# A hybrid RWKV-7/Hyena block on one core: a fixed order of products in the first stage, low halves on VectorE, and low-rank weights a block ahead

## The chip, the cores and the metric

The kernel runs on one core of one Trainium2 chip. The metric is the time of one execution in microseconds (us). TensorE (PE) multiplies, VectorE (DVE), ScalarE (ACT) and GpSimd (POOL) work on elements, and SyncE (SP) issues most DMA transfers, GpSimd some.

## What is computed

A block of two layers on a latent sequence of 256 tokens and a context of 256 tokens, 2048 channels, float32. Layer 0 mixes tokens with RWKV-7, layer 1 with a Hyena convolution; a squared-ReLU MLP follows each. Only the front of layer 0 is touched here:

```python
mod  = (silu(c) @ ada_w[i] + ada_b[i])          # 6 x 2048; shift mod[0], scale mod[1]; modc from c_ctx
h    = modulate(rms_norm(x, norm_g), mod[0], mod[1])
xx   = shift_grid(h) - h                        # neighbour token, minus the token
xw, xk, xa = h + xx*mu[1], h + xx*mu[2], h + xx*mu[4]      # and mu[0], mu[3], mu[5] for r, v, gate
lw   = dec_w0 + tanh(xw @ dec_w1) @ dec_w2      # two directions, rank 96
a    = sigmoid(a0 + (xa @ a1) @ a2)             # two directions, rank 96
g    = sigmoid((h + xx*mu[5]) @ g1) @ g2        # latent only, rank 256
k, v, r = xk @ w_k, xv @ w_v, xr @ w_r          # 2048 x 2048
kk   = k*k_k ; kk = kk * rsqrt(sum(kk*kk, per head))       # then the scan over tokens
```

## The kernel before, in words

Channels lie on partitions, in 16 tiles k of 128; the 512 columns of a tile are 256 context and 256 latent tokens. A float32 product is made as three products of split halves (`mm3`): ScalarE casts the high half (`xh`, `wh`, `l2h`), a subtraction gives the low half (`xl`, `wl`, `l2l`), and PE adds high·high, low·high and high·low. `split_into` makes both halves; its `eng` says which engine subtracts, VectorE by default.

**First stage** (`start`, 0 to about 198 us). It needs shift and scale of layer 0, 2048 channels each, which come in four quarters q of 512 channels. `ada_first(ch, q)` loads eight weight tiles `aw` of 512 KB for one of the two, multiplies each with silu(c) on PE (L288), copies the sum (`rows`), turns it with the small `pick` products (L294), and VectorE adds the bias (`mod`, `modc`). `rwkv_h(q)` then scales four tiles of `hall` on ScalarE. For each of these k, `shifted` builds `sx` (shifted minus own token; ScalarE, then two VectorE additions), and `mix_split` builds four mixtures `xt` on VectorE (mu indices 1, 4, 5 and 2; index 5 on the latent half, 256 columns) with halves `xh` and `xl`. Indices 1, 4 and 5 go into the first low-rank products (12 `mm` and 6 `sg` matmuls a k); index 2 is kept for the product with w_k. `ONPOOL` puts all `xl` on GpSimd, through L172. In `start`, the order of an engine's queue is set by a scheduler with priorities (`high_priority`); code marked by pins (`self.pins`, `pin`) keeps the order in which it is written.

**Second stage** (`rwkv_proj`, to 457 us): the 2048 x 2048 product with w_k, and beside it 44 of the 80 units of `lora2`, the second low-rank products, the mixtures of r and v, and `ada_run`, the rest of layer 0's modulation (`aw` tiles of 256 KB, added up in `acc` on VectorE or GpSimd). For each of 16 row tiles the square `ksq` is split, `ksh` on ScalarE and `ksl` on GpSimd, and summed per head by two `sg` products (L743).

**Third stage** (`rwkv_begin`, 457 to 590 us): `scan_prepare(0)`, a chain of small steps that ends in an inverse by substitution (31 steps of `d` and `tmp` on VectorE), the fills of r and v (`fl` products; `fx` loaded from GpSimd's queue, `fr` from SyncE's), and the remaining 36 units of `lora2`, the last 16 of them the eight gate blocks. The scan's first products, `sc<-VU,NT`, follow. In `lora2` the tiles `raw`, `l2h` and `l2l` have one buffer each; a block's load, its two halves and its products follow one another.

Of the kernel before, what the change touches and what calls it, by code (L numbers as in the profile page):

```python
# [69 lines left out]
class Kern:  # L70
# [42 lines left out]
    pins = None  # L113

# [162 lines left out]
    def ada_first(self, ch, i, pool):  # L277
# [5 lines left out]
        for k in range(0, KT, 2):  # L283
            w = pool.tile([P, 2, 512], F32, name="aw", bufs=self.AW)
            nc.sync.dma_start(w, self.I["ada_w"][0, k * P : (k + 2) * P, c0 : c0 + 512].rearrange("(a p) n -> p a n", p=P))
            for a in range(2):
                j = (k + a) % 4
                nc.tensor.matmul(ps[32 * j : 32 * j + 32, :], lhsT=self.wide[:, k + a, :], rhs=w[:, a],  # L288
                                 start=k < 4, stop=k >= KT - 4, tile_position=(0, 32 * j))
# [3 lines left out]
        for b in range(4):  # L293
            nc.tensor.matmul(tp[:, b, :], lhsT=rows[:, b * P : (b + 1) * P], rhs=self.pick, start=True, stop=True)  # L294
# [3 lines left out]
    def ada_run(self, n, pool, psum="mm", on_pool=True, per=2, bufs=2):  # L298
# [308 lines left out]
    def rwkv_h(self, xp, q):  # L607

        nc = self.nc
        for st in range(2):  # L610
            hv = self.hview(st)
            gs = xp.tile([P, 16], F32, name=f"gs{st}", bufs=1)
            cs = slice(4 * q, 4 * q + 4)
            scl = self.modc[:, 1, cs] if st == 0 else self.mod[:, 0, 1, cs]
            nc.vector.scalar_tensor_tensor(gs[:, cs], scl, 1.0, self.col("norm_g", 4 * q, 4), op0=ALU.add, op1=ALU.mult)
            for k in range(4 * q, 4 * q + 4):
                sh = self.modc[:, 0, k : k + 1] if st == 0 else self.mod[:, 0, 0, k : k + 1]
                nc.scalar.activation(hv[:, k, :], hv[:, k, :], AF.Identity, scale=gs[:, k : k + 1], bias=sh)
# [60 lines left out]
    def lora2(self, pool):  # L679
# [5 lines left out]
        block = lambda: (pool.tile([P, 512], t, name=n, bufs=1) for t, n in ((F32, "raw"), (F32R, "l2h"), (F32R, "l2l")))  # L685
        for q in range(4):
            for nm, e in (("dec", 0), ("dec", 1), ("a", 0), ("a", 1)):
                b0 = self.hw0 if nm == "dec" else self.ha0
                r, hi, lo = block()
                nc.sync.dma_start(r[:RANK], I[f"{nm}_w2"][0, e][:, q * 512 : (q + 1) * 512])  # L690
                w = self.split_into(hi[:RANK], r[:RANK], lo[:RANK])
                for j in range(4):
# [3 lines left out]
                    t = pool.tile([P, 512], F32, name="l2t")  # L696
                    nc.scalar.activation(t, ps, AF.Tanh, scale=0.5, bias=b0[:, e * 16 + m : e * 16 + m + 1])
                    (nc.gpsimd if m % 4 < self.LPOOL else nc.vector).tensor_scalar(t, t, 0.5, 0.5, op0=ALU.mult, op1=ALU.add)
                    if nm == "dec":
                        u = pool.tile([P, 512], F32, name="l2u")  # L700
# [5 lines left out]
        for q in range(8):  # L706
            r, hi, lo = block()
            nc.sync.dma_start(r[:].rearrange("p (k n) -> p k n", k=2),
                              I["g_w2"][0][:, q * 256 : (q + 1) * 256].rearrange("(k p) n -> p k n", p=P))
            w = self.split_into(hi[:], r[:], lo[:])  # L710
            for j in range(2):
# [4 lines left out]
                t = pool.tile([P, 512], F32, name="l2t")  # L716
# [4 lines left out]
    def rwkv_proj(self, l2, ad1):  # L721
        nc, tc, I = self.nc, self.tc, self.I
        ev = self.ev
        ad = self.ada_run(self.ADA[0], ad1, "sg", self.ONP[0], 1, 2)
# [8 lines left out]
        def evk(m, ps):  # L733
# [7 lines left out]
            self.split_into(sh[:], s[:], sl[:], nc.gpsimd)  # L741
# [753 lines left out]
    ONPOOL = {1: 4, 4: 4, 5: 4, 2: 4}  # L1495
# [131 lines left out]
    def start(self, ap, xp):  # L1627
# [15 lines left out]
        for ch in range(2):  # L1643
            self.ada_first(ch, 0, ap)
        acc = [self.mm.tile([P, 512], F32, name="mm") for _ in range(4)]
        gacc = [self.sg.tile([P, 512], F32, name="sg") for _ in range(2)]
        for q in range(4):
            w, wg = weights(q)
            if q < 3:
                with self.tc.high_priority(self.PRA):  # L1650
                    for ch in range(2):
                        self.ada_first(ch, q + 1, ap)
            with self.tc.high_priority(self.PRH):
                self.rwkv_h(ap, q)
            self.xs = self.xs if q else []
            for k in range(4 * q, 4 * q + 4):
                sx = self.shifted(k)
# [177 lines left out]
```

## Time and profile before

| | |
|---|---|
| median of three runs | 3630.55 us (3610.51 to 3632.46) |
| profiled execution | 3626.62 us, its span 3623.9 us |
| PE busy | 3349.5 us (92%) |
| DVE, ACT, POOL busy | 2474.2 us (68%), 1740.7 us (48%), 551.9 us (15%) |
| mean granted PE clock | 0.965 of full speed |
| moved by DMA | 836.78 MB, mean 231 GB/s |

Times inside the span are counted from its start. Busy shares are means over stages of different kinds; the three stages above are the first 16% of the span.

### The profile page before, as it was taken

What the parts mean: (1) busy time and instruction counts of PE and PEld (TensorE: products, weight loads), DVE (VectorE), ACT (ScalarE), POOL (GpSimd) and SP (SyncE); (2) the same over time, 40 slices, a digit from 0 to 9 for tenths busy, and PEclk for the clock granted to TensorE, in tenths of its full rate; (3) what the DMA queues carried; (4) which work ended last, traced back from release to release, by engine and by line L of the source; (5) the groups of instructions that cost most, each with busy time, mean ns of one, the idle gap of its engine ahead of it and who ended that gap; (6) DMA issues with size and microseconds to landing.
All of it is one profiled execution on the core that took longest, in us unless ns stands there. A gap on an engine that the chain in (4) does not pass through costs nothing. (4 is left out here: it accounts for less than half of the span.)

```text
span 3623.9 us, 74582 instructions
## 1 busy us (share of the span) xinstructions
PE 3349.5 (92%) x30598; PEld 2912.4 (80%) x30598; DVE 2474.2 (68%) x3787; ACT 1740.7 (48%) x3069; POOL 551.9 (15%) x576
## 2 busy tenths in 40 slices
PE   7798877989999878999999999999999899999999
PEld 3376666878888756798988889899997798989897
DVE  5888675777777755587777776587787685555554
ACT  4444344444554544444434335576564664435343
POOL 2632221111111000000000002044441540000000
PEclk9989988999999989999999999999999999999999
DMA  9668798888899735688888887476665776555553
GB/s 328 203 211 268 238 293 253 272 267 272 272 281 276 224 126 168 202 257 288 255 271 277 283 264 240 158 238 214 213 211 176 241 251 197 178 189 182 192 181 126
DMA packets 587806, 836.78 MB, mean 231 GB/s; under 512 B 39551, under 2 KB 373280, under 8 KB 587464
## 3 DMA queue, kind: packets, MB, share of 16 engines
q1 hardware_dynamic: 556360, 718.76, 62.0%
q0 software_dynamic: 31104, 113.26, 9.9%
q8 instruction: 239, 3.92, 0.4%
q14 instruction: 103, 0.84, 0.1%
HBM read 777.31 MB, written 54.59 MB: 230 GB/s over the span
## 5 line engine op out<-in xcount | busy, mean ns | idle before, releaser
L53 DVE TENSOR_TENSOR wl<-w,wh 128x1024 fp32r<-128x1024 f32 (+1 forms) x716 | 919.6, 1290 | 541.1 <-ACT wh L53 537.8
L53 ACT CAST wh<-w 128x1024 fp32r<-128x1024 f32 (+1 forms) x716 | 737.7, 1043 | 728.8 <-PE mm L111 416.4
L111 PE MATMUL mm<-hxh,wh 128*128 128x258 f32 x2816 | 805.3, 287 | 13.2 <-DVE nt L53 11.4
L111 PE MATMUL mm<-hxh,wl 128*128 128x258 f32 x2816 | 803.9, 286 | 5.5 <-DVE wl L53 5.5
L111 PE MATMUL mm<-hxl,wh 128*128 128x258 f32 x2816 | 801.1, 285 | 0.0
L111 PEld LDWEIGHTS mm<-hxh,wh 128*128 128x128 f32 x2816 | 536.3, 191 | 17.4 <-DVE nt L53 13.5
L111 PEld LDWEIGHTS mm<-hxh,wl 128*128 128x128 f32 x2816 | 536.0, 190 | 8.5 <-DVE wl L53 7.2
L111 PEld LDWEIGHTS mm<-hxl,wh 128*128 128x128 f32 x2816 | 538.6, 191 | 1.8
L322 POOL TENSOR_TENSOR acc<-acc,aw 128x512 f32<-128x512 f32 x180 | 274.2, 1523 | 1360.7 <-ACT aw L53 1259.3
L111 PE MATMUL mm<-wh,uh 128*128 128x512 f32 x1024 | 405.8, 396 | 1.2 <-DVE nt L53 1.2
L111 PE MATMUL mm<-wl,uh 128*128 128x512 f32 x1024 | 400.2, 391 | 4.0 <-DVE wl L53 4.0
L111 PE MATMUL mm<-wh,ul 128*128 128x512 f32 x1024 | 402.6, 393 | 0.0
L53 DVE SCALAR_TENSOR_TENSOR acc<-aw,sc,acc 128x512 f32<-128x512 f32 x300 | 233.4, 778 | 101.0 <-DMA aw<-in_ada_w 98.5
L111 PEld LDWEIGHTS mm<-wl,uh 128*128 128x128 f32 x1024 | 192.6, 188 | 49.0 <-DVE wl L53 6.2
L111 PEld LDWEIGHTS mm<-wh,ul 128*128 128x128 f32 x1024 | 192.2, 188 | 45.6
L111 PEld LDWEIGHTS mm<-wh,uh 128*128 128x128 f32 x1024 | 192.6, 188 | 42.3 <-DVE nt L53 1.8
L111 PE MATMUL fl<-fh,fx 128*128 128x256 f32 x1024 | 213.1, 297 | 10.1 <-DMA fx<-xv 8.6
L111 PEld LDWEIGHTS fl<-fh,fx 128*128 128x128 f32 x1024 | 168.6, 194 | 28.1 <-issue 14.1
L53 ACT ACTIVATE aw<-aw,sc 128x512 f32<-128x512 f32 x180 | 125.7, 719 | 130.7 <-DMA aw<-in_ada_w 129.6
L111 PE MATMUL fl<-flo,fx 128*128 128x256 f32 x512 | 146.4, 286 | 0.0
L111 PE MATMUL mm<-xh,wh 128*128 128x512 f32 (+1 forms) x320 | 126.8, 416 | 17.5 <-ACT xh L53 14.1
L111 PE MATMUL sg<-ard,KB 64*64 64x64 f32 (+1 forms) x3584 | 130.4, 247 | 11.2 <-DVE NT L53 3.7
(352 smaller groups left out, 6016.3 us busy)
## 6 DMA issues: line engine op xcount, KB each, us to landing
aw<-in_ada_w SPq DMA_DIRECT2D x288, 512.0 KB, 5.7
w<-in_mlp_down SPq DMA_DIRECT2D x128, 1024.0 KB, 5.2
w<-in_mlp_up SPq DMA_DIRECT2D x120, 1024.0 KB, 6.1
fx<-xv POOLq DMA_DIRECT2D x128, 512.0 KB, 6.2
aw<-in_ada_w SPq DMA_DIRECT2D x192, 256.0 KB, 3.1
w<-in_hy_in_w SPq DMA_DIRECT2D x44, 1024.0 KB, 5.9
fx<-xr POOLq DMA_DIRECT2D x64, 512.0 KB, 5.8
w<-in_w_k SPq DMA_DIRECT2D x16, 1024.0 KB, 5.7
```

Source lines behind the costliest of these rows:

```text
L53: return self.kern.pin(self.key, f(*a, **kw))
L111: return self.pin("pe", self.nc.tensor.matmul(out, lhsT=lhsT, rhs=rhs, **kw))
L322: nc.gpsimd.tensor_tensor(acc, acc, w[:, a], op=ALU.add)
```

## The change

- The first stage is written so that PE's order is fixed (pins for PE alone): per k, up to six `aw` tiles of the next quarter and then the 18 products of k. `rwkv_h` yields after each k.
- `ONPOOL` becomes 0 for all, and `ksl` loses its `nc.gpsimd`: 64 `xl` and 16 `ksl` subtractions move from GpSimd to VectorE.
- `lora2` loads `raw` one block ahead, or two when its buffers are doubled; in `rwkv_begin` its tiles come from a pool of their own, "l2b", with two buffers for `raw`, `l2h`, `l2l` and three for `l2t`, `l2u`.
- `ada_run`'s loads in the second stage are issued under `issue_after(self.mixed)`, the last `xl` of the first stage.

```diff
@@ pin
-        if self.pins is not None:
+        if self.pins is not None and key in self.pinned:
@@ split_into
-        (eng or self.nc.vector).tensor_tensor(lo, f32, hi, op=ALU.subtract)
+        self.split_last = (eng or self.nc.vector).tensor_tensor(lo, f32, hi, op=ALU.subtract)
@@ ada_first: nc.tensor.matmul becomes self.product, and after each aw tile
+            yield
@@ ada_run
+                with self.tc.issue_after(behind) if behind else ExitStack():
+                    nc.sync.dma_start(w, ...)
@@ rwkv_h
+        for k in range(4 * q, 4 * q + 4):
+            for st in range(2):
...
+                nc.scalar.activation(hv[:, k, :], hv[:, k, :], AF.Identity, scale=gs[st][:, k : k + 1], bias=sh)
+            yield
@@ lora2
-        block = lambda: (pool.tile([P, 512], t, name=n, bufs=1) for t, n in ((F32, "raw"), (F32R, "l2h"), (F32R, "l2l")))
+        self.l2p = pool, 1
+        def blocks():
...
+            load(*todo.pop(0))
+            while raws:
+                r, n = raws.pop(0)
+                p, b = self.l2p
+                hi, lo = (p.tile([P, 512], F32R, name=nm, bufs=b) for nm in ("l2h", "l2l"))
+                w = self.split_into(hi[:n], r[:n], lo[:n])
+                while todo and len(raws) < b:
+                    load(*todo.pop(0))
+                yield w
@@ rwkv_proj
-            self.split_into(sh[:], s[:], sl[:], nc.gpsimd)
+            self.split_into(sh[:], s[:], sl[:])
@@
-    ONPOOL = {1: 4, 4: 4, 5: 4, 2: 4}
+    ONPOOL = {1: 0, 4: 0, 5: 0, 2: 0}
@@ start
+        self.pins, self.pinned = {}, ("pe",)
+        ada = lambda q: itertools.chain(self.ada_first(0, q, ap), self.ada_first(1, q, ap))
...
             for k in range(4 * q, 4 * q + 4):
+                with self.tc.high_priority(self.PRH):
+                    next(h)
+                with self.tc.high_priority(self.PRA):
+                    for _ in itertools.islice(nxt, 6 if k % 4 < 3 else 99):
+                        pass
                 sx = self.shifted(k)
...
+        self.mixed = self.split_last.ins
@@
-                self.rwkv_begin()
+                with ExitStack() as e3:
+                    self.l2p = self.pool(e3, "l2b", 3), 2
+                    self.rwkv_begin()
```

PE in the first stage, before: the last two `aw` tiles of quarter 3 (`aw_1059`, `aw_1063`) stand between the products of the last k of quarter 2 (`mm_369` to `sg_374` are the six sums).

```order
L288 MATMUL sc_1034<-aw_1059,wide_139 32x512 x2
L111 MATMUL sg_373<-xh_1255,wh_988 128x256
L111 MATMUL sg_374<-xh_1255,wh_988 128x256
L111 MATMUL mm_369<-xl_1230,wh_978 96x512
L111 MATMUL mm_369<-xh_1231,wl_979 96x512
L111 MATMUL mm_370<-xl_1230,wh_978 96x512
L111 MATMUL mm_370<-xh_1231,wl_979 96x512
L288 MATMUL sc_1034<-aw_1063,wide_139 32x512 x2
```

The same place after, from the last product of the second k of quarter 2:

```order
L111 MATMUL sg_374<-xh_1134,wl_989 128x256
L111 MATMUL sc_1088<-aw_1153,wide_139 32x512 x2
L111 MATMUL sc_1088<-aw_1157,wide_139 32x512 x2
L111 MATMUL sc_1088<-aw_1161,wide_139 32x512 x2
L111 MATMUL sc_1088<-aw_1165,wide_139 32x512 x2
L111 MATMUL sc_1171<-pick_143,rows_1169 128x2 x4
L111 MATMUL mm_369<-xh_1183,wh_978 96x512
L111 MATMUL mm_369<-xl_1182,wh_978 96x512
L111 MATMUL mm_369<-xh_1183,wl_979 96x512
```

The last four tiles of quarter 3 and the turn by `pick` now stand in one run, two k's of products ahead of the end of quarter 2, and the three products of a tile follow one another.

VectorE at the end of the first stage, before (`xt` mixtures, `sx` the shift; `acc` adds up layer 0's other modulation, which is work of the second stage):

```order
L53 SCALAR_TENSOR_TENSOR acc_1620<-aw_1659,sc2_92,acc_1620 128x512
L53 SCALAR_TENSOR_TENSOR xt_1413<-sx_1395,cols_71,hall_126 128x512
L53 TENSOR_TENSOR sx_1441<-sx_1441,hall_126 128x255
L53 TENSOR_TENSOR sx_1441<-sx_1441,hall_126 128x192
L53 SCALAR_TENSOR_TENSOR acc_1620<-aw_1730,sc2_92,acc_1620 128x512
L53 SCALAR_TENSOR_TENSOR xt_1425<-sx_1395,cols_71,hall_126 128x256
L53 SCALAR_TENSOR_TENSOR xt_1437<-sx_1395,cols_71,hall_126 128x512
L53 SCALAR_TENSOR_TENSOR acc_1620<-aw_1743,sc2_92,acc_1620 128x512
L53 SCALAR_TENSOR_TENSOR xt_1447<-sx_1441,cols_71,hall_126 128x512
L53 SCALAR_TENSOR_TENSOR acc_1620<-aw_1754,sc2_92,acc_1620 128x512
```

and after, up to the last `xl` (`wl` is a low half of w_k):

```order
L53 SCALAR_TENSOR_TENSOR acc_1622<-aw_1775,sc2_92,acc_1622 128x512
L53 SCALAR_TENSOR_TENSOR xt_1459<-sx_1441,cols_71,hall_126 128x512
L53 TENSOR_TENSOR xl_1433<-xt_1435,xh_1434 128x512
L53 SCALAR_TENSOR_TENSOR acc_1622<-aw_1870,sc2_92,acc_1622 128x512
L53 TENSOR_TENSOR xl_1445<-xt_1447,xh_1446 128x512
L53 SCALAR_TENSOR_TENSOR xt_1471<-sx_1441,cols_71,hall_126 128x256
L53 SCALAR_TENSOR_TENSOR acc_1622<-aw_1881,sc2_92,acc_1622 128x512
L53 TENSOR_TENSOR xl_1457<-xt_1459,xh_1458 128x512
L53 SCALAR_TENSOR_TENSOR xt_1483<-sx_1441,cols_71,hall_126 128x512
L53 TENSOR_TENSOR xl_1469<-xt_1471,xh_1470 128x256
L53 SCALAR_TENSOR_TENSOR acc_1622<-aw_1894,sc2_92,acc_1622 128x512
L53 TENSOR_TENSOR wl_1546<-w_1543,wh_1545 128x1024
```

The `xl` now stand in VectorE's queue behind their `xt`, and the `acc` additions still stand there among them, ahead of the last `xl`.

PE at the end of `rwkv_begin`, before: the last of three gate blocks (products of `hh_g`, `hl_g` with `l2h`, `l2l`, 12 a block) that stand between the last fill product and the scan.

```order
L111 MATMUL sc_5042<-hl_g0_1521,l2h_5007 128x256
L111 MATMUL sc_5012<-hh_g0_1522,l2l_5008 128x256
L111 MATMUL sc_5012<-hh_g1_1529,l2h_5007 128x256
L111 MATMUL sc_5012<-hl_g1_1528,l2h_5007 128x256
L111 MATMUL sc_5012<-hh_g1_1529,l2l_5008 128x256
L111 MATMUL sc_5042<-hh_g0_1522,l2l_5008 128x256
L111 MATMUL sc_5042<-hh_g1_1529,l2h_5007 128x256
L111 MATMUL sc_5042<-hl_g1_1528,l2h_5007 128x256
L111 MATMUL sc_5042<-hh_g1_1529,l2l_5008 128x256
L111 MATMUL sc_5161<-VU_5150,NT_5082 64x64 x8
```

and after, half a gate block and what follows it:

```order
L111 MATMUL sg_5089<-ard0_3605,KB_3705 64x64
L111 MATMUL sc_5045<-hh_g0_1522,l2h_5011 128x256
L111 MATMUL sc_5045<-hl_g0_1521,l2h_5011 128x256
L111 MATMUL sc_5045<-hh_g0_1522,l2l_5012 128x256
L111 MATMUL sc_5045<-hh_g1_1529,l2h_5011 128x256
L111 MATMUL sc_5045<-hl_g1_1528,l2h_5011 128x256
L111 MATMUL sc_5045<-hh_g1_1529,l2l_5012 128x256
L111 MATMUL sg_5088<-ard0_3605,KB_3705 64x64 x2
L111 MATMUL sg_5089<-ard0_3605,KB_3705 64x64
L111 MATMUL sg_5090<-ard0_3605,KB_3705 64x64
L111 MATMUL fl_4774<-fx_5003,fh_4999 128x256 x2
L111 MATMUL fl_4774<-fx_5003,flo_5000 128x256
```

Behind the last row come three more such fill groups, four of the next fill, and then `sc_5165<-VU_5154,NT_5086`. Gate products now stand between fills (`fl`), and none in a row ahead of the scan; from the end of the inverse (`d,d`) to the scan PE has 48 fill and 18 gate products after, 24 and 48 before, and 24 of `ard`, `KB` in both.

## Rows read from the trace of the kernel before

**Rows 1.** Busy time by stretches in the first stage; columns: stretch, length, busy us of PE, PEld, DVE, ACT, POOL (instructions), granted PE clock, DMA share, GB/s.

```profile
50.00:100.00 50.00, 47.27 (x243) 20.18 (x239) 36.14 (x49) 27.64 (x51) 29.39 (x21) 0.97 0.94 317
...
150.00:200.00 50.00, 29.46 (x101) 18.41 (x100) 41.44 (x51) 25.49 (x42) 27.20 (x18) 0.70 0.41 120
```

**Rows 2.** VectorE in order of time, 50 to 200 us: each quarter's `mod`; columns: start us, us, instruction [idle before <- releaser].

```profile
52.54 0.16 DVE L53 TENSOR_TENSOR mod<-sc,cols 128x4 f32<-128x4 f32 x1 [8.84 <-PE sc L294]
...
83.06 0.15 DVE L53 TENSOR_TENSOR mod<-sc,cols 128x4 f32<-128x4 f32 x1
...
113.64 0.15 DVE L53 TENSOR_TENSOR mod<-sc,cols 128x4 f32<-128x4 f32 x1
...
154.47 0.16 DVE L53 TENSOR_TENSOR mod<-sc,cols 128x4 f32<-128x4 f32 x1
```

**Rows 3.** Groups of instructions by line and shape, 0 to 200 us; columns: busy us, mean ns of one, idle before and releasers.

```profile
L172 POOL TENSOR_TENSOR xl<-xt,xh 128x512 fp32r<-128x512 f32 x48 | 75.9, 1598 | 93.5 <-ACT xh L53 92.3
L53 DVE SCALAR_TENSOR_TENSOR xt<-sx,cols,hall 128x512 f32<-128x512 f32 x48 | 57.2, 1225 | 2.9 <-POOL xl L172 2.8
```

**Rows 4.** PE in order of time at the end of quarter 2.

```profile
148.67 1.05 PE L288 MATMUL sc<-aw,wide 128*32 128x512 f32 x4
149.65 0.50 PE L111 MATMUL sg<-xh,wh 128*128 128x256 f32 x2
149.99 0.40 PE L111 MATMUL mm<-xl,wh 128*96 128x512 f32 x1
150.23 0.40 PE L111 MATMUL mm<-xh,wl 128*96 128x512 f32 x1
...
153.48 0.95 PE L294 MATMUL sc<-pick,rows 128*128 128x2 f32 x8
```

**Rows 5.** VectorE in order of time in the last quarter of the first stage.

```profile
159.45 1.04 DVE L53 TENSOR_TENSOR sx<-sx,hall 128x255 f32<-128x255 f32 x3 [2.87 <-ACT sx L53]
...
175.55 0.74 DVE L53 SCALAR_TENSOR_TENSOR acc<-aw,sc,acc 128x512 f32<-128x512 f32 x1
176.22 1.40 DVE L53 SCALAR_TENSOR_TENSOR xt<-sx,cols,hall 128x512 f32<-128x512 f32 x2
```

**Rows 6.** PE in order of time, the last product of the first stage and the first with w_k.

```profile
195.14 0.28 PE L111 MATMUL sg<-xh,wl 128*128 128x256 f32 x1
198.71 0.79 PE L111 MATMUL mm<-xh,wh 128*128 128x512 f32 x1 [3.29 <-ACT xt L53]
```

**Rows 7.** VectorE in order of time in the second stage.

```profile
446.15 0.68 DVE L53 TENSOR_TENSOR KB<-a,ei 128x512 f32<-128x512 f32 x1
446.74 0.69 DVE L53 TENSOR_TENSOR ard<-id,eend 128x512 f32<-128x512 f32 x1
```

**Rows 8.** Second stage, 199 to 457 us, a group of GpSimd's instructions, columns as in rows 3.

```profile
L172 POOL TENSOR_TENSOR ksl<-ksq,ksh 128x512 fp32r<-128x512 f32 x16 | 28.8, 1803 | 33.1 <-ACT ksh L53 32.6 <-PE sg L743 0.4
```

**Rows 9.** Second stage, waits of PE: us in total, times, longest.

```profile
PE sg L743 <- POOL ksl L172: 2.3, 3, 1.2
```

**Rows 10.** Third stage, 457 to 592 us, waits of PE, in the same columns.

```profile
PE sc L111 <- ACT l2t L53: 12.4, 5, 4.5
PE sc L111 <- ACT l2h L53: 10.6, 4, 3.8
PE fl L111 <- DMA fx<-xr: 3.7, 3, 1.5
```

**Rows 11.** Third stage and a stretch of it, columns as in rows 1.

```profile
457.00:590.00 133.00, 99.01 (x965) 88.47 (x965) 84.77 (x151) 56.56 (x108) 24.79 (x42) 0.86 0.92 286
470.00:550.00 80.00, 59.88 (x478) 52.87 (x478) 61.04 (x122) 32.63 (x65) 17.90 (x31) 0.91 1.01 318
```

**Rows 12.** PE in order of time, from the end of the inverse to the first product of the scan.

```profile
566.81 0.23 PE L111 MATMUL sg<-d,d 32*32 32x32 f32 x4
...
567.54 0.28 PE L111 MATMUL sc<-hl_g,l2h 128*128 128x256 f32 x1
567.66 0.28 PE L111 MATMUL sc<-hh_g,l2l 128*128 128x256 f32 x1
...
574.74 0.63 PE L111 MATMUL fl<-fx,fh 128*128 128x256 f32 x2
575.16 0.41 PE L111 MATMUL fl<-fx,flo 128*128 128x256 f32 x1
578.70 0.58 PE L111 MATMUL sc<-hh_g,l2h 128*128 128x256 f32 x1 [3.12 <-ACT l2h L53]
...
583.77 0.58 PE L111 MATMUL sc<-hh_g,l2h 128*128 128x256 f32 x1 [2.14 <-ACT l2h L53]
...
588.17 0.39 PE L111 MATMUL sc<-hh_g,l2h 128*128 128x256 f32 x1 [1.47 <-ACT l2h L53]
...
590.15 0.62 PE L111 MATMUL sc<-VU,NT 64*64 64x64 f32 x14
```

**Rows 13.** VectorE in order of time, the last steps of the inverse.

```profile
548.91 0.22 DVE L53 TENSOR_TENSOR d<-d,tmp 128x60 f32<-128x60 f32 x1
552.49 0.69 DVE L53 TENSOR_TENSOR flo<-fr,fh 128x512 fp32r<-128x512 f32 x1 [3.36 <-ACT fh L53]
...
554.22 0.18 DVE L53 TENSOR_TENSOR d<-d,tmp 128x31 f32<-128x31 f32 x1
```

More of the change, by code (lines that the diff above doesn't have):

```diff
@@ L293, in ada_first, with ada_run @@
         for b in range(4):
-            nc.tensor.matmul(tp[:, b, :], lhsT=rows[:, b * P : (b + 1) * P], rhs=self.pick, start=True, stop=True)
+            self.product(tp[:, b, :], rows[:, b * P : (b + 1) * P], self.pick, start=True, stop=True)
         for q, dst in enumerate((self.mod[:, 0, ch], self.modc[:, ch])):
             nc.vector.tensor_tensor(dst[:, 4 * i : 4 * i + 4], tp[:, :, q], self.col("ada_b", ch * 16 + 4 * i, 4), op=ALU.add)
-    def ada_run(self, n, pool, psum="mm", on_pool=True, per=2, bufs=2):
+    def ada_run(self, n, pool, psum="mm", on_pool=True, per=2, bufs=2, behind=None):
         nc = self.nc
@@ L684, in lora2, with load @@
         nc.vector.memset(bm[:, 0:513:64], 0.0)
-        block = lambda: (pool.tile([P, 512], t, name=n, bufs=1) for t, n in ((F32, "raw"), (F32R, "l2h"), (F32R, "l2l")))
+        self.l2p = pool, 1
+        def blocks():
+            raws = []
+            def load(nm, e, q):
+                p, b = self.l2p
+                r = p.tile([P, 512], F32, name="raw", bufs=b)
+                if nm == "g":
+                    nc.sync.dma_start(r[:].rearrange("p (k n) -> p k n", k=2),
+                                      I["g_w2"][0][:, q * 256 : (q + 1) * 256].rearrange("(k p) n -> p k n", p=P))
+                else:
+                    nc.sync.dma_start(r[:RANK], I[f"{nm}_w2"][0, e][:, q * 512 : (q + 1) * 512])
+                raws.append((r, P if nm == "g" else RANK))
+            todo = [(nm, e, q) for q in range(4) for nm in ("dec", "a") for e in range(2)] + [("g", 0, q) for q in range(8)]
+            load(*todo.pop(0))
+            while raws:
+                r, n = raws.pop(0)
+                p, b = self.l2p
+                hi, lo = (p.tile([P, 512], F32R, name=nm, bufs=b) for nm in ("l2h", "l2l"))
[3 more added lines that the diff above has]
+                yield w
+        block = blocks()
         for q in range(4):
@@ L706, in lora2 @@
         for q in range(8):
[L707 to L710, printed above, removed]
+            w = next(block)
             for j in range(2):
@@ L715, in lora2 @@
                     self.mm3(ps[:, :L], self.cut(w, slice(k * 256 + j * P, k * 256 + (j + 1) * P)), self.lora["g", k], k == 0, k == 1)
[L716 removed]
+                t = self.l2p[0].tile([P, 512], F32, name="l2t")
                 nc.scalar.copy(t[:, :L], ps[:, :L])
@@ L1648, in start @@
             w, wg = weights(q)
[L1649 to L1654, printed above, removed]
+            nxt = ada(q + 1) if q < 3 else iter(())
+            h = self.rwkv_h(ap, q)
             self.xs = self.xs if q else []
             for k in range(4 * q, 4 * q + 4):
+                with self.tc.high_priority(self.PRH):
+                    next(h)
+                with self.tc.high_priority(self.PRA):
+                    for _ in itertools.islice(nxt, 6 if k % 4 < 3 else 99):
+                        pass
                 sx = self.shifted(k)
```

31 lines of the change are left out of this document (14 added, 17 removed).

## The prediction

> **What bounds the kernel now.** I read the busy times by stretches first, then the groups of instructions by shape, then each engine in order of time where the change acts. From 50 to 100 us PE is busy 47.27 of 50 us and the DMA moves 317 GB/s at a share of 0.94; from 150 to 200 us PE is busy only 29.46 us, at a granted clock of 0.70, while VectorE is busy 41.44 us [rows 1]. So the first stage is held by loads and PE at first and by VectorE at its end. The modulation of the four quarters is ready at 52.54, 83.06, 113.64 and 154.47 us [rows 2]: two gaps of 30.5 us and one of 40.8. The last product of the stage starts at 195.14, 40.7 us behind the last modulation, and the product with w_k starts at 198.71 [rows 6]. The third stage takes 457 to 590 us. There PE waits 12.4 us for `l2t` and 10.6 us for `l2h` [rows 10], with a DMA share of 0.92 and 286 GB/s on average [rows 11], and its end is three gate blocks, each behind a wait: 3.12, 2.14 and 1.47 us [rows 12]. All later stages run one behind the other, so what these give or take at 590 us I carry unchanged to the end.
>
> **First stage: the quarters.** The prices come from PE in order of time [rows 4]: an `aw` tile takes 0.98 us (148.67 to 149.65), a matmul of 512 columns 0.24 us (149.99 to 150.23), `pick` 0.95 us. A k has 12 matmuls of 512 columns and 6 of 256, which I price at half: 12 x 0.24 + 6 x 0.12 = 3.6 us. In the fixed order PE does this from one modulation to the next: two k's left over (7.2 us), six tiles (5.9), a k (3.6), two tiles, a wait for `rows` of about 1 us, and `pick` (3.9), four tiles (3.9), a k (3.6), four tiles, `rows` and `pick` again (5.9). That is 34.0 us. The second left-over k is not ready when PE reaches it: its casts stand on ScalarE behind eight scalings of `hall` and a `sx`, and those take 5 us (154.47 to 159.45, where VectorE's wait for `sx` ends [rows 2, 5]), while the first left-over k covers only 3.6; with some 0.9 us behind it for its cast and its `xl`, I add 5.0 + 0.9 - 3.6 = 2.3 us. A quarter is then 36.3 us. The first quarter has no left-over k and stays with the loads, 30.5 us. So the last modulation comes at 52.54 + 30.5 + 2 x 36.3 = 155.6 us, against 154.47: +1.1 us. The gain of the `aw` tiles in front, which before ran at 148.67 and later, is paid back by products that now can't slip behind a waiting one.
>
> **First stage: its end.** Here VectorE decides, and every `xl` is now its work. One pass over 512 columns costs it 0.67 us beside nothing (175.55 to 176.22 [rows 5]) and a subtraction of two tiles 0.59 us (446.15 to 446.74 [rows 7]); I take 0.61. From the first `sx` of quarter 3 to the last `xl`, the changed order has 13 `xt` and 12 `acc` (25 x 0.67 = 16.8), 15 `xl` (9.2), nine `xt` and `xl` of 256 columns (3.3), eight additions to `sx` (2.6), four `wl` of 576 to 1024 columns (4.3 at 0.61 per 512) and an `l2l` (0.6): 36.8 us. PE doesn't need the last `xl`, nor the two instructions ahead of it, which leaves 34.4 us; with 5.0 us ahead for `hall` and `sx` and some 0.7 us of products behind, the stage ends 40.1 us after the last modulation, against 40.7. Before, the `xt` took 1225 ns on average beside GpSimd's `xl` of 1598 ns [rows 3]: that slowing goes, 0.55 us for each `xt`, and the 0.61 us of an `xl` takes its place. Sum of the stage: +1.1 - 0.6, which I call **0 us**. Bounds: if PE never starves in a quarter (34.0 us each) -5 us (twice 2.3); if a quarter takes 40.8 like the slowest one before, +9 us.
>
> That the `acc` stay in this sum is a reading of the order, not of the diff. `issue_after(self.mixed)` holds loads on SyncE behind an instruction of VectorE, and the order shows `acc` among the last `xt` and `xl` as before.
>
> **Second stage.** Sixteen `ksl` of 1803 ns on GpSimd [rows 8] become 16 of 0.61 us on VectorE, 9.8 us more for an engine that has room. PE waited 2.3 us for `ksl` [rows 9]. What can be won is that, and what VectorE's queue may cost is each `ksl` behind one longer instruction, about 0.3 us for 16: I take **-1 us**, from -2.3 to +4. The loads of `raw` a block ahead bring nothing here, where halves have one buffer.
>
> **Third stage.** Two buffers for the halves, three for `l2t` and a load two blocks ahead take away what PE waits for. Three sums bound the gain. By PE's waits it is at most 12.4 + 10.6 = 23 us [rows 10]. By the chain: from the end of the inverse (566.81) to the scan PE now has 48 fill, 18 gate and 24 small products. At 0.12 us for one of 256 columns (567.54 to 567.66) that is 66 x 0.12 + 1.2 = 9.1 us, and the scan starts at 575.9 instead of 590.15: -14.2 us. At 0.21 us (574.74 to 575.16 for two of them, where the clock is at its lower level) it is 15.1 us: -8.2 [rows 12]. The inverse itself can end earlier: from 548.91 to 554.22 VectorE stands in front of a fill's half for 3.36 us and behind an `l2l` before its last step [rows 13], up to 4.5 us more. By the loads: 133 us at 286 GB/s are 38.0 MB, and at the 318 GB/s of the densest long stretch, whose share is 1.01 [rows 11], they take 119.6 us, so no more than 13.4 us can go. I take **-13 us**, the lowest of these that isn't a case of a slow clock, and for the range -5 (half of the waits come back as waits for `fx`, of which `xr` alone already has 3.7 us [rows 10]) to -20.
>
> The page "DMA: Bandwidth & Descriptors" of the Trainium skill says (Issuing engines are not separate DMA queues) that transfers issued by different engines run on the same 16 DMA engines and interleave, so a load that is issued earlier only takes its turn earlier. It also gives about 358 GB/s as the bound from memory for one core (Where 436 GB/s comes from); by that the 38.0 MB would take an estimated 106 us, and 27 us could go. The rows show 318 at a full share, and I keep to them.
>
> **Sum.** 3626.62 + 0 - 1 - 13 = 3612.6 us, which I give as **3613**. It stands against the profiled execution; the median of the runs shown is 3630.55, 4 us above it, and against that the change is -0.5%. About 1%, 36 us, is what a measurement of this kernel can tell from no change.
>
> **Rivals.**
> 1. *The first stage is freed.* If the `acc` left its end (the loads held behind the last `xl`, as the code names it), 12 x 0.67 = 8 us go; with quarters at 34.0 us another 5, and with the third stage at its best, -20: 3626.6 - 8 - 5 - 1 - 20 = 3593 us. Against it: the `acc` stand in the order.
> 2. *The third stage is bound by its fills.* The gate products move between the fills, but `fx` comes no faster, and what PE doesn't wait at the end it waits ahead of fills: -4, in all 3622 us. For it: the DMA share of 1.01 from 470 to 550 us.
> 3. *Slower: PE's fixed order waits at every quarter.* Where a k's `xl` isn't there, nothing else can run. The place is the two left-over k's and the k behind the six tiles. If VectorE, which takes its work in order too, brings the `xl` 2 us late for each of the four k's, a quarter is 44.3 us: two of them +16, the first and the end of the stage +4 each, and 3626.6 + 0.5 + 24 - 14 = 3637 us. It decides from a quarter of about 41 us on (three times 4.5 us are the 14 us that the rest gives). Against it: VectorE's work in a quarter is some 27 us by the same prices.
> 4. *The move does nothing for the time.* The `xl` and `ksl` were no one's wait; the third stage gains 13 and VectorE's 80 new subtractions (80 x 0.61 = 49 us of work) cost as much where it decides: 3627 us.
>
> **Chances and range.** Forecast 0.50, rival 1 0.15, rival 2 0.15, rival 3 0.12, rival 4 0.08. The forecast's own range is 3600 (-5, -2.3, -20) to 3635 (+9, +4, -5). Rival 1 ends at 3593, near the mark of 1% at 3590; with the inverse ending earlier as well it is past it, so I count most of it as faster. Rival 3 passes the upper mark, 3663, only where the lateness is twice as large; I give that half of it. With a little for what I don't see, faster by over 1% has 0.15, slower by over 1% 0.08, between 0.77. The range for eight in ten takes in rivals 1 to 3 at their prices: 3592 to 3640.
>
> **What would show it.** In the changed profile: no `xl` and no `ksl` on GpSimd; `xt` near 0.7 us; the modulation at about 83, 119 and 156 us; the last product of the first stage near 195; the first product with w_k near 199; fewer than 10 us of PE's waits for `l2t` and `l2h` in the third stage; the third stage some 120 us long, not 133. I would be wrong if a quarter takes 41 us or 31 us, if `xl` costs VectorE over 0.9 us, or if the waits for `fx` grow by more than 8 us.

## The result, and the profile after

The changed kernel takes 3597.11 us (median, 3585.96 to 3607.2) and the kernel before, timed beside it, 3614.71 (3604.6 to 3632.46). The ratio is 0.994, with a 95% interval of 0.9919 to 0.9962: 18 us by the medians and 22 by the ratio, some 0.6%, are gone. The forecast was 3613 us and a change of -0.5% against the median then known. The profiled execution after took 3607.2 us, with this span:

```profile
span 3605.3 us, 74531 instructions
PE 3326.2 (92%) x30598; PEld 2904.8 (81%) x30598; DVE 2457.0 (68%) x3867; ACT 1739.7 (48%) x3069; POOL 435.0 (12%) x496
```

**First stage.** The stretches of [rows 1] in the kernel after, in the same columns, and one more:

```profile
50.00:100.00 50.00, 42.54 (x216) 22.18 (x210) 32.93 (x70) 27.95 (x52) 0.00 (x0) 0.84 0.74 261
100.00:150.00 50.00, 41.39 (x206) 20.27 (x206) 34.82 (x70) 22.27 (x41) 0.00 (x0) 0.97 0.86 287
150.00:200.00 50.00, 30.70 (x129) 20.75 (x130) 42.03 (x75) 28.89 (x50) 0.00 (x0) 0.90 0.45 136
```

GpSimd is empty in these stretches, and from 50 to 100 us PE is less busy than it was (42.54 of 50 us, before 47.27). VectorE's modulation, which answers to [rows 2], the two groups of [rows 3], and the end of the stage on PE, as in [rows 6]:

```profile
81.11 0.16 DVE L53 TENSOR_TENSOR mod<-sc,cols 128x4 f32<-128x4 f32 x1 [1.42 <-PE sc L111]
...
117.28 0.16 DVE L53 TENSOR_TENSOR mod<-sc,cols 128x4 f32<-128x4 f32 x1 [3.65 <-PE sc L111]
...
153.25 0.16 DVE L53 TENSOR_TENSOR mod<-sc,cols 128x4 f32<-128x4 f32 x1 [4.07 <-PE sc L111]
```

```profile
L53 DVE SCALAR_TENSOR_TENSOR xt<-sx,cols,hall 128x512 f32<-128x512 f32 x48 | 34.7, 744 | 0.0
L53 DVE TENSOR_TENSOR xl<-xt,xh 128x512 fp32r<-128x512 f32 x48 | 32.5, 683 | 12.6 <-ACT xh L53 12.6
```

```profile
193.17 0.28 PE L111 MATMUL sg<-xh,wl 128*128 128x256 f32 x1
196.50 0.79 PE L111 MATMUL mm<-xh,wh 128*128 128x512 f32 x1 [3.05 <-ACT xt L53]
```

The first modulation is at 54.28 us, so the quarters take 26.8, 36.2 and 36.0 us. `xt` fell from 1225 to 744 ns, `xl` is now 683 ns of VectorE, and the stage ends 2 us earlier.

PE in the quarter that ends at 153.25 us: six `aw` tiles in one run (four matmul rows a tile), the next product, the first of the last four tiles, and `pick`; then PE's wait for `aw` in this quarter (117.28 to 153.25 us), columns as in [rows 9]:

```profile
127.05 2.78 PE L111 MATMUL sc<-aw,wide 128*32 128x512 f32 x24
129.77 0.47 PE L111 MATMUL mm<-xh,wh 128*96 128x512 f32 x1
...
146.06 1.05 PE L111 MATMUL sc<-aw,wide 128*32 128x512 f32 x4 [1.03 <-DMA aw<-in_ada_w]
...
152.16 1.05 PE L111 MATMUL sc<-pick,rows 128*128 128x2 f32 x8 [0.69 <-ACT rows L53]
```

```profile
PE sc L111 <- DMA aw<-in_ada_w: 2.9, 6, 1.0
```

**Third stage.** PE's waits from 457 to 592 us after, in the columns of [rows 10]; then the stage as one stretch, as in [rows 11]; then PE where the scan begins, as at the end of [rows 12]:

```profile
PE sc L111 <- ACT l2t L53: 12.7, 6, 3.3
PE sc L111 <- DMA VU<-v: 7.5, 1, 7.5
...
PE fl L111 <- DMA fx<-xv: 1.5, 1, 1.5
```

```profile
439.60:562.80 123.20, 95.39 (x976) 85.70 (x976) 85.69 (x153) 58.77 (x113) 27.30 (x44) 0.92 0.97 307
```

```profile
554.88 0.45 PE L111 MATMUL sg<-ard,KB 64*64 64x64 f32 x12
562.83 1.04 PE L111 MATMUL sc<-VU,NT 64*64 64x64 f32 x12 [7.49 <-DMA VU<-v]
```

The waits for `l2h` are gone and the three gate blocks no longer stand at the end; the scan's first product now waits 7.49 us for its own operand `VU`.

### The profile page after: what moved, and what is told of

Read it like the earlier page. It is cut to its first block, busy times and chain, and to the rows that moved or that the text cites. A ratio compares the mean times of both kernels' runs of the same rounds, so it can differ in the third digit from the quotient of the medians.

```text
span 3605.3 us, 74531 instructions
## 1 busy us (share of the span) xinstructions
PE 3326.2 (92%) x30598; PEld 2904.8 (81%) x30598; DVE 2457.0 (68%) x3867; ACT 1739.7 (48%) x3069; POOL 435.0 (12%) x496
## 4 chain that ended last, share of the span: by engine, by line
PE 49%; DMA 21%; DVE 14%; ACT 6%; issue 6%; POOL 2%; SPq 1%; ACTq 0%; DVEq 0%; POOLq 0%
PE mm L111 34%; DMA aw<-in_ada_w 10%; PE fl L111 5%; PE sg L111 5%; PE sc L111 4%; DVE wl L53 3%; DMA w<-in_mlp_down 2%; DVE acc L53 2%; DMA w<-in_mlp_up 2%; POOL acc L325 2%; ACT wh L53 2%; DVE tmp L53 1%; ACT aw L53 1%; DVE d L53 1%; DMA a<-a 1%
## 5 line engine op out<-in xcount | busy, mean ns | idle before, releaser
L111 PEld LDWEIGHTS mm<-hxh,wl 128*128 128x128 f32 x2816 | 534.1, 190 | 10.7 <-DVE wl L53 9.3
L53 DVE SCALAR_TENSOR_TENSOR acc<-aw,sc,acc 128x512 f32<-128x512 f32 x300 | 225.3, 751 | 89.6 <-DMA aw<-in_ada_w 87.0
L111 PE MATMUL mm<-xl,wh 128*128 128x512 f32 (+1 forms) x320 | 131.7, 412 | 12.1 <-DVE xl L53 12.0
```

The source lines that it names most:

```text
L53: return self.kern.pin(self.key, f(*a, **kw))
L111: return self.pin("pe", self.nc.tensor.matmul(out, lhsT=lhsT, rhs=rhs, **kw))
```

## The experiments

All kernels compute the whole result. The table gives each kernel's stages from one profile each, in us: the first product with w_k (end of the first stage), from there to the sums of heads (`kt`, second stage), to the first `sc<-VU,NT` (third stage), to the first product of the output projection (scan), and the rest up to PE's last product, with the median time and the ratio to the kernel before with its interval. Each ratio is to the kernel before timed beside that kernel, whose medians lie between 3613.87 and 3618.54 us.

```
                     w_k   second  third   scan    rest   median   ratio
before              198.7  258.9  132.5   838.9  2191.0  3614.71
before, again       200.3  253.3  126.4   834.5  2187.9
after               196.5  243.1  123.2   847.5  2191.1  3597.11  0.9940 (0.9919-0.9962)
after, again        199.9  244.8  121.3   827.9  2193.3
e1_ksl_pool         197.2  251.5  119.6   842.2  2185.9  3602.50  0.9953 (0.9935-0.9971)
e2_low_only         199.9  252.0  118.5   843.3  2196.4  3611.59  0.9980 (0.9967-0.9993)
e3_first_only       198.3  254.5  128.7   829.0  2184.3  3606.32  0.9969 (0.9953-0.9986)
e4_ahead_single     195.8  245.0  132.6   832.9  2188.1  3598.05  0.9935 (0.9917-0.9954)
e4 again            197.6  245.9  131.3   838.9  2186.5  3601.53  0.9962 (0.9944-0.9980)
e5_acc_behind       190.1  255.2  117.3   839.5  2195.9  3601.80  0.9938 (0.9909-0.9968)
e6_xl_pool          218.4  247.3  120.6   840.3  2200.9  3621.35  1.0020 (1.0000-1.0040)
e7_no_pins          188.1  243.4  119.0   847.1  2187.1  3586.50  0.9914 (0.9884-0.9943)
e9_pool_two         195.5  246.6  121.3   840.8  2188.8  3598.24  0.9936 (0.9913-0.9958)
e10_both_two        197.5  243.9  115.5   847.0  2192.9  3593.07  0.9924 (0.9898-0.9950)
```

**The parts apart.** Four kernels take the change to pieces. e1 is after with one part undone:

```
-            self.split_into(sh[:], s[:], sl[:])
+            self.split_into(sh[:], s[:], sl[:], nc.gpsimd)
```

> The change with ksl back on GpSimd, nothing else. Theory 1: in the second stage PE waited 7.5 us for ksl on VectorE, where it stands behind the preparation of the scan, and 2.3 us on GpSimd before; so the second stage is 3 to 6 us shorter than after the change (237 to 240 us), and the whole 2 to 6 us faster than it. Rival 2: GpSimd's ksl slows VectorE's two-input work; second stage 246 to 252 us, the whole 3 to 8 us slower than the change. Rival 4: it makes no difference of more than 2 us, since another wait ends last in each place.

It is 0.9953, in the whole time not told apart from after. The second stage is 251.5 us, 8.4 more than after: the move of `ksl` is worth about that there. Theory 1 had the sign wrong. Rival 2 had the size right; whether its reason holds is asked by e9 below.

e2 is the kernel before with the new `lora2` and its pool alone:

```
+                with ExitStack() as e3:
+                    self.l2p = self.pool(e3, "l2b", 3), 2
+                    self.rwkv_begin()
```

> The kernel before with the new lora2 alone (loads of raw ahead, and the pool of two and three buffers in rwkv_begin); first stage, xl and ksl as before. Theory 1 (the gain behind the first stage is lora2's: raw loads no longer stand in SyncE's queue behind the stores of the block before, and PE doesn't wait for halves): the first product with w_k at 198 to 200 us as before, from there to the head sums 242 to 249 us (258.9 before, 243.1 after the change), from the head sums to the scan 121 to 127 us (132.5 and 123.2), in all 12 to 18 us faster than before (ratio 0.995 to 0.9965). Rival 2 (the second stage is shorter because xl and ksl left GpSimd, whose work slowed VectorE): second stage 256 to 260 us, third 121 to 127, in all 6 to 10 us faster.

It is 0.998: the third stage falls to 118.5 us, some 10 less, but the scan is 843.3, and the whole kernel wins 7 us. Its second stage, 252.0 us, stays where GpSimd's `ksl` has it, against theory 1.

e3 is the first stage's part alone: after, with `lora2` as before, no `l2b` and `ksl` on GpSimd.

> The change without lora2's part and with ksl on GpSimd again: the fixed order of the first stage and xl on VectorE alone. Theory 1: first product with w_k at 195 to 198 us, from there to the head sums 256 to 261 us, third stage 130 to 135 us, in all 0 to 4 us faster than before (ratio 0.999 to 1.000). Rival 2: second stage 243 to 250 us, in all 10 us or more faster. Rival 3 (the scan gives back what starts earlier): the 2 us are gone by the end of the scan.

It is 0.9969. The end of the first stage shows only a microsecond or two of the 11 us that this ratio means; the rest doesn't lie in one stage and I can't place it. The execution that was profiled, 3600.62 us, is one of this kernel's fastest (median 3606.32), and its scan and rest are short.

e4 is after without the pool of its own, so that loads run ahead but each tile keeps its old buffers:

```
-                with ExitStack() as e3:
-                    self.l2p = self.pool(e3, "l2b", 3), 2
-                    self.rwkv_begin()
+                self.rwkv_begin()
```

> The change without the pool of rwkv_begin: raw is loaded one block ahead everywhere, but raw, l2h and l2l keep one buffer and l2t, l2u the buffers they had. If the order of the loads gives the third stage's gain: third stage 122 to 126 us as after the change (123.2), the whole as the change within 3 us. If the buffers give it: third stage 129 to 134 us, the gate blocks again in a row ahead of the scan, and the whole 6 to 10 us slower than the change, 8 to 12 us faster than before. The second stage is 242 to 245 us in both cases.

Its third stage is 132.6 us, as before the change, and PE's waits there are the old ones:

```profile
PE sc L111 <- ACT l2t L53: 13.1, 5, 3.6
PE sc L111 <- ACT l2h L53: 9.0, 5, 4.6
```

So loading one block ahead gives nothing in that stage; the pool gives it, which means the second buffers and the second block ahead that they let in, not told apart here. Yet the whole kernel, 0.9935, is as fast as after, against the expectation: its scan is 832.9 us.

Of the readings that these four set against one another, that the gain is that of the loads and buffers of `lora2` holds for 7 of some 20 us only; that low halves leaving GpSimd pay is right for `ksl`, with 8 us in its stage; that the scan gives some of it back is suggested by e2 and, the other way round, by e4, and is asked again below. No run takes the loads under `issue_after` apart.

**What varies by itself.** Two profiles of the same kernels:

> The kernel before, unchanged, profiled a second time, to see how much a stage varies from one execution to the next. The one profile so far has the second stage at 258.9 us, the third at 132.5, the scan at 838.9, and its span of 3623.9 us lies high among its own times. The kernels that share its second stage's order of casts (the one with the low ranks alone, the one with the first stage alone) have 252.0 and 254.5. Theory: the second stage is again 250 to 259 us, so that 4 to 8 us of the difference to the kernel after are the edit's and the rest is chance; the scan is 829 to 839. Rival: the stages come out within 1 us of the first profile, and then the whole 15.8 us that the second stage lost is the change's.

> The kernel after, unchanged, profiled a second time. First profile: second stage 243.1 us, third 123.2, scan 847.5, span 3605.3. Theory: second stage 242 to 246 again (it was 245.0 in the kernel that differs only in the low ranks' buffers); the scan is 838 to 848 and takes up what the third stage won, whatever that is, so that it ends within 5 us of 1408. Rival: the scan is near 833, as in two other kernels, and ends near 1396; then the longer scan was chance and not the price of the earlier start.

The second stage repeats within 2 us after and within 6 before, the third within 2 and 6; the scan varies by 20 us in one and the same kernel (847.5 and 827.9). A difference in the scan can be read from means over several profiles only. The kernel before came out as its theory said (253.3 and 834.5 us). For the kernel after the rival came true in this profile: the scan was short and ended at 1393.9 us.

**Where the second stage's gain comes from.** Five profiles with `ksl` on GpSimd and one `ksq` have a second stage of 251.5 to 258.9 us, mean 254.0 (before twice, e1, e2, e3); six with `ksl` on VectorE have 243.1 to 247.3, mean 244.9 (after twice, e4 twice, e6, e7). That is 9 us, while PE waited only 2.3 us for GpSimd's `ksl` [rows 9]. PE's waits in the second stage, e1 and then after:

```profile
PE sg L770 <- ACT ksh L53: 10.5, 5, 3.3
PE sc L111 <- ACT l2h L53: 6.4, 3, 3.5
...
PE sg L770 <- POOL ksl L173: 2.0, 2, 1.3
```

```profile
PE sg L770 <- DVE ksl L53: 7.5, 4, 2.8
PE sg L770 <- ACT ksh L53: 4.4, 3, 1.9
...
PE sc L111 <- ACT l2h L53: 2.2, 1, 2.2
```

What falls is the wait for ScalarE's casts `ksh` and `l2h`, from 16.9 to 6.6 us; the wait for `ksl` itself grows. ScalarE's groups say why its casts were late. The first line is e1, the second after, the third e9:

```profile
L53 ACT ACTIVATE ksq<-mm,cols 128x512 f32<-128x512 f32 x16 | 11.0, 685 | 23.0 <-DVE kt L53 15.4 <-POOL ksl L173 7.6
```

```profile
L53 ACT ACTIVATE ksq<-mm,cols 128x512 f32<-128x512 f32 x16 | 11.0, 686 | 17.5 <-DVE kt L53 11.8 <-DVE ksl L53 5.7
```

```profile
L53 ACT ACTIVATE ksq<-mm,cols 128x512 f32<-128x512 f32 x16 | 10.9, 685 | 10.7 <-DVE kt L53 10.6
```

`ksq` has one buffer. The next square waits on ScalarE until `ksl` has read the last one (7.6 us in e1), and the casts queued behind it wait too. The square's other wait, for `kt`, falls as well, from 15.4 to 11.8 us; why is not shown. e9 leaves `ksl` on GpSimd and gives `ksq` a second buffer:

```
 (on top of e1; kt, in both of its places, falls from three buffers to two)
-            s = ev.tile([P, 512], F32, name="ksq", bufs=1)
+            s = ev.tile([P, 512], F32, name="ksq", bufs=2)
```

> The kernel after with the low half of k squared (ksl) back on GpSimd, as in the kernel before, but with two buffers for the square (ksq); one buffer of the rows of k (kt) is given up for the room. With one buffer, ScalarE, which works in order, waits for GpSimd's ksl to release ksq (7.5 us over five waits in its row), and the casts of the low ranks' weights and of ksh stand behind it. Theory A (the single buffer, held for the length of ksl, is what the second stage pays for GpSimd): the second stage falls from 251.5 us to 243 to 247, close to the 243.1 with ksl on VectorE, and the whole time from 3602.5 to about 3597. Rival B (GpSimd's access beside VectorE slows VectorE, or PE's own wait for ksl decides): it stays at 250 to 253 us and the whole time at 3602. If a wait for kt appears, the giving up of its buffer is seen there and the run says little.

The second stage is 246.6 us, below all five profiles with one buffer, with `ksl` still on GpSimd at 1828 ns: 7 of the 9 us come back against their mean, and 5 of 8 against e1, from which this edit starts. In its one profile the wait of the square for `ksl` is gone. So theory A holds for the stage: the held buffer is the cause of most of its gain, and what is left, some 2 to 4 us, is open. The whole time isn't told apart from e1's. The same edit on the kernel after:

> The kernel after, ksl on VectorE as there, and two buffers for the square of k (ksq), one fewer for kt. If what GpSimd's ksl cost was the time that it held ksq, VectorE's ksl holds it too, for a shorter time (ScalarE waits 5.7 us for it over the stage): the second stage falls from 243 to 245 us by another 2 to 4 us, to 240 to 243, and the whole time to 3593. Rival: PE is busy 228 of its 243 us there, and its remaining waits (ksl 7.5, ksh 4.4 us) are for the chain of casts itself and not for a buffer: it stays at 243 to 245 and 3597.

Here it brings nothing in its stage (243.9 us): the rival was right, and what VectorE's `ksl` holds back on ScalarE costs the stage nothing. The whole time of 3593.07 us isn't told apart from after's.

**The first stage's end.** e5 keeps the work and holds the first `acc` of each sum behind the last subtraction of the stage:

```
                         r = nc.vector.tensor_scalar(acc, w[:, a], s, None, op0=ALU.mult)
+                        if behind and last is None:
+                            self.tc.add_manual_dep(r.ins, behind.name, ...)
```

> The kernel after, with the 12 acc of VectorE that start the sums of the next modulation held behind the last subtraction of the first stage in VectorE's order, as the order of their loads would suggest. My reading of the first stage's end: VectorE sets it, 12 acc of 0.67 us stand in its way, and without them it ends up to 8.0 us earlier: the last product starts at 185 to 188 us, not 193.2, with the first product of w_k at about 189. Rival: acc fill gaps of VectorE behind a wait for sx or PE sets the end; the last product starts at 191 to 194 and the whole time stays at 3597 +- 4. Where the end moves but the second stage takes the acc up, its length grows from 243 to 248 or more and the whole time stays too.

PE at the end of its first stage, and its largest wait in the second:

```profile
186.68 0.28 PE L111 MATMUL sg<-xh,wl 128*128 128x256 f32 x1
190.09 0.50 PE L111 MATMUL mm<-xh,wh 128*128 128x512 f32 x1 [3.13 <-ACT xt L53]
```

```profile
PE sc L111 <- ACT l2h L53: 8.5, 3, 3.9
```

The last product starts at 186.68 us: up to 8.0 us less had been expected, and 6.5 came. The second stage gives it back: 255.2 us instead of 244.9, with PE waiting 8.5 us for `l2h` where it waited 2.2. The time is after's.

**The fixed order, and GpSimd.** e6 is after with `xl` back on GpSimd; e7 is after without the fixed order:

```
e6:
-    ONPOOL = {1: 0, 4: 0, 5: 0, 2: 0}
+    ONPOOL = {1: 4, 4: 4, 5: 4, 2: 4}
e7:
-        self.pins, self.pinned = {}, ("pe",)
+        self.pins, self.pinned = None, ("pe",)
```

> The kernel after with the low halves of the first stage's activations (xl of the products with the five ranks) back on GpSimd, the fixed order of products and the modulation in front kept. Theory (my prices: beside GpSimd's xl of 1.6 to 1.8 us VectorE's xt costs 1.2 us, and alone xt and xl together 0.74 + 0.68): the two ways cost VectorE about the same, 1.2 against 1.4 us each, but a fixed order of products waits for each xl, which now comes 1.7 us behind xh and not 0.7; PE's waits for xl grow from 12 to 20 us, a quarter takes 38 to 40 us instead of 36, and the first product with w_k comes at 199 to 206 instead of 195.5 to 199.9. Whole time 3600 to 3605. Rival: GpSimd's xl runs beside VectorE at no cost, the last product comes earlier because VectorE sets the end of the stage and has 15 x 0.68 us less to do: w_k at 190 to 194.

> The kernel after without the fixed order of PE's products in the first stage: the scheduler again chooses which product comes next, as in the kernel before; everything else as after. Theory: the order is worth about what it costs, first product with w_k at 195 to 200 (after 196.5 and 199.9 in two profiles), whole time 3592 to 3602. Rival A (the fixed order makes PE wait at each quarter, up to 12 us for xl): without it the stage is 5 to 8 us shorter, w_k at 189 to 193. Rival B (the order brings the modulation forward and is what pays for the low halves on VectorE): without it the modulation of the last quarter comes after 156 us and w_k after 202.

In e6 the theory had the right sign, but 21 us came where some 5 had been expected. In e7 its rival A is right: 9 us, where it said 5 to 8, though not for the reason that it gave, as the waits show. The stage ends 21 us later in e6 and 9 us earlier in e7, one profile each, than in the kernels that share after's first stage (mean of eight profiles 197.3 us). Two groups of e6 answer to [rows 3]:

```profile
L173 POOL TENSOR_TENSOR xl<-xt,xh 128x512 fp32r<-128x512 f32 x48 | 77.7, 1631 | 119.0 <-ACT xh L53 116.7 <-PE sg L111 1.5
L53 DVE SCALAR_TENSOR_TENSOR xt<-sx,cols,hall 128x512 f32<-128x512 f32 x48 | 57.2, 1223 | 28.8 <-POOL xl L173 28.8
```

e7's last modulation is at 144.87 us, after's at 153.25. From the first modulation to the last, as one stretch each, after and then e7:

```profile
54.28:153.25 98.97, 82.48 (x421) 41.80 (x422) 67.75 (x139) 50.21 (x92) 0.00 (x0) 0.92 0.76 260
```

```profile
54.02:144.87 90.85, 88.39 (x430) 39.67 (x431) 68.11 (x139) 50.63 (x93) 0.00 (x0) 0.97 0.86 282
```

PE's waits in these two stretches, after and then e7:

```profile
PE sc L111 <- DMA aw<-in_ada_w: 6.3, 11, 1.5
PE mm L111 <- ACT xh L53: 4.3, 3, 2.4
PE sc L111 <- ACT rows L53: 4.2, 6, 0.7
PE mm L111 <- DVE xl L53: 1.1, 3, 0.5
```

```profile
PE sc L111 <- ACT rows L53: 1.1, 2, 0.7
PE mm L111 <- ACT xh L53: 1.0, 1, 1.0
PE sc L111 <- DMA aw<-in_ada_w: 0.4, 1, 0.4
```

From the last modulation to the first product with w_k, after and then e7, and PE's longest wait there in after:

```profile
153.25:196.50 43.25, 25.06 (x108) 16.70 (x107) 38.53 (x71) 24.82 (x42) 0.00 (x0) 0.92 0.46 139
```

```profile
144.87:188.09 43.22, 25.05 (x101) 16.94 (x99) 39.40 (x73) 23.93 (x41) 0.00 (x0) 0.84 0.49 145
```

```profile
PE mm L111 <- DVE xl L53: 10.8, 6, 3.5
```

All that the fixed order costs lies ahead of the last modulation. There PE is idle for 16.5 us with it and for 2.5 without, where another product is taken meanwhile. What it waits for are loads of `aw` and ScalarE's `xh` and `rows`; the `xl` are about 1 us of it. Behind the last modulation PE waits 10.8 us for `xl`, and this costs nothing: both kernels take 43.2 us there, with VectorE busy for some 39. The largest of after's waits in this stage is the one that doesn't matter.

e6's last modulation is at 168.99 us, so that 16 of its 22 us against after's profile lie ahead of it too. Its waits from 50 to 199 us have `rows` first, and those for `xl` don't reach the 20 us that the theory had:

```profile
PE sc L111 <- ACT rows L53: 12.4, 7, 4.5
PE mm L111 <- POOL xl L173: 10.4, 7, 5.7
```

So the first stage's parts are large and of opposite sign. With the scheduler's order, `xl` on VectorE and the new modulation loop bring 11.5 us (199.6, mean of before twice and e2, to 188.1); the fixed order then costs 9. What the 11.5 us are made of is not shown: no kernel has the new loop alone, and before, PE waited only 3.5 us for GpSimd's `xl` in this stage. With `xl` on GpSimd, the new loop and the fixed order together cost 19 us (199.6 to 218.4). e7 has the shortest median of all, 3586.5 us and 0.9914, but its interval overlaps that of after.

**Whether the scan gives back the start.** e4, profiled a second time:

> The kernel after with the low ranks' weights loaded a block ahead but in the old single buffers (two for the results), run again for a second profile: in the first, the third stage took 132.6 us, as before the change, and the scan 832.9, and the whole time was 3598.05, like after. Theory C (the scan gives back most of what the buffers win): again a third stage of 127 to 133 us, a scan of 828 to 835, and a whole time of 3594 to 3600. Rival D (chance: the buffers are worth their 9 us in the third stage down to the end): the scan is 838 to 845 this time and the whole time 3602 to 3608.

This doesn't decide. The third stage, 131.3 us, is as theory C has it, the scan, 838.9, as rival D has it, and the time, 3601.53, lies between their ranges. Over all profiles the five without buffers of their own have a third stage of 130.3 us and a scan of 834.8, the nine with them 119.6 and 841.7. Of 10.7 us won, 6.9 would thus be given back. But the scans of the two groups overlap (829.0 to 838.9 and 827.9 to 847.5), and by their scatter the difference is anything from 1 to 13 us (my estimate of a 95% interval). Part of it is PE's speed: for the same number of products its busy time in the scan is 742.8 us without the buffers and 747.4 with. The scan of e4, of after and of e7 as one stretch each, in the columns of [rows 1]:

```profile
573.40:1406.20 832.80, 740.20 (x14483) 636.36 (x14482) 572.39 (x1231) 406.39 (x961) 92.27 (x171) 0.95 0.79 240
```

```profile
562.80:1410.40 847.60, 747.40 (x14483) 643.12 (x14483) 572.01 (x1231) 406.91 (x960) 92.42 (x171) 0.94 0.78 237
```

```profile
550.50:1397.50 847.00, 752.12 (x14482) 648.48 (x14482) 572.64 (x1230) 406.81 (x960) 92.25 (x171) 0.94 0.77 238
```

Over the fourteen profiles the granted clock is 0.95 or 0.96 in the scans of up to 835 us and 0.93 or 0.94 in those of 847 us and more. What lowers it, and whether the earlier start does, stays open: "after, again" starts its scan early too, and has 0.96 and 827.9 us.

## Why the prediction was right, and where it was not

The sign was the forecast one, and as a change -18 us came for -14. The time of 3597.11 us lies in the range for eight in ten (3592 to 3640), but near its lower end; it is under the forecast's own range (3600 to 3635) and nearer to rival 1's 3593 than to 3613, though not by rival 1's way. Among the terms the second stage failed and the unchanged scan is in doubt, in opposite directions, and the quarters came right by errors that cancel. That the sum came so close is in part luck.

- **Quarters: the length right, two of its terms not.** Modulation was forecast at 83.1, 119.4 and 155.6 us and came at 81.1, 117.3 and 153.3; a quarter of 36.3 us measured 36.2 and 36.0. But six `aw` tiles were to take 5.9 us at 0.98 us each, the price of a tile between other products [rows 4]; in one run they took 2.7, from 127.05 to 129.77 us. And the last four tiles with `rows` and `pick`, also at 5.9, took 8.2, because PE waited for loads of `aw`, a wait that the working had at nothing. The first quarter took 26.8 us, not 30.5.
- **End of the stage: right.** 40.1 us forecast from the last modulation to the last product, 39.9 measured. That VectorE sets it and that the `acc` stand in it was shown by e5, and by e7, which needs the same time there in another order of PE. The prices held nearly: an `xl` is 0.683 us long in the trace, an `xt` 0.744, and they follow one another at the 0.6 and 0.67 us of the working.
- **Sum of the stage: right, at -2.3 us for 0** (197.3 against 199.6). What the working didn't ask is what each part is worth alone. Rival 3, the fixed order waiting at every quarter, had the mechanism in kind: it costs 9 us (e7). But PE waits there for `aw`, `xh` and `rows`, and hardly for the `xl` that rival 3 named, and its price was too high. The gain that pays for it, 11.5 us, stood nowhere as a gain: the working only set 0.55 us of slowing against 0.61 us of an `xl` on VectorE.
- **Second stage: the step that failed.** -1 us forecast, with -2.3 as the lower bound; -9 came. The bound was read from the row in which PE waits for GpSimd's `ksl` [rows 9]. The price of a slow `ksl` [rows 8] was for the most part paid elsewhere: it held `ksq`, ScalarE stood still for it, and PE's waits were booked under `ksh` and `l2h`. A wait row names the last link and not the cause, so it is no bound.
- **Third stage: right in kind, a little large.** -13 forecast, -9.3 in the first profile and -10.7 over all. The waits for `l2h` went as said, and those for `fx` didn't grow. Those for `l2t` stayed at 12.7 us, where fewer than 10 were forecast for both, and 7.5 us for `VU<-v` were new. The bound by the loads, 119.6 us, was none: four of the nine stages with the pool are under it, and e10's of 115.5 us moved, at 317 GB/s, an estimated 36.6 MB and not 38.0.
- **Carried unchanged: in doubt.** The scan is on average 6.9 us longer where it starts earlier, with the scatter said above. The rest varies from 2184 to 2201 us and is taken as unchanged.
- **The base.** The forecast of 3613 stood on a profiled execution of 3626.62 us, and the kernel before turned out to lie at 3614.71. This accounts for 12 of the 16 us between forecast and result; the change itself, -14, came out as -18.

The four stage differences, -2.3, -9.1, -10.7 and +6.9, make -15, inside the interval of the ratio (-14 to -29 us) and near its small end. Rival 1 fell: the `acc` stayed, and where e5 moved them the second stage took them up. Rival 2 fell, `fx` was no bound. Rival 4 fell: `ksl` was no one's long wait and still cost 9 us.

## What to carry to other kernels

Where an operand with a single buffer is read by a slow engine, look at what the writer's queue holds behind it: the price shows as waits for other tiles of the writing engine, and a second buffer may bring most of what a faster reader brings (5 to 7 of some 9 us here). A fixed order on PE is priced by taking it away: with it each late operand stops PE, and here it cost 9 us that a gain beside it hid. Ask of a wait whether another engine sets the length of its stretch anyway: 10.8 us of waiting for `xl` cost nothing here. When the whole shows little, ask for each part alone before calling the parts small.

## What the runs showed of the hardware

VectorE's `xt` takes 1225 and 1223 ns while GpSimd subtracts beside it (before, e6) and 744 ns when GpSimd is empty. The Trainium skill, page "SBUF — State Buffer" (SBUF: two separate sides), says that a VectorE instruction with two inputs in SBUF and a GpSimd instruction that reads SBUF shut each other out for a whole instruction instead of sharing. That agrees in direction; the mean of 0.48 us that is lost is less than a third of GpSimd's 1631 ns, so most `xt` weren't kept waiting for a whole one. Before, the longest took 1828 ns, 1.1 us more than alone.

The same 14,483 products of the scan keep PE busy from 738 to 752 us in fourteen profiles, at granted clocks of 0.93 to 0.96 of full speed. These 14 us are more than the third stage's whole gain.
